# Modulation vectors: each finished half written to its row in DRAM by one four-partition transfer, two pieces later

## The chip, the cores and the metric

One core of one Trainium2 chip runs the whole program. The time is device microseconds of one execution. PE is TensorE's matrix multiplication, PEld its weight load, DVE VectorE, ACT ScalarE, POOL GpSimd, and SP the engine that issues most of the transfers. TensorE's clock is granted at one of two levels, 1.2 and 2.4 GHz; the profile writes it as a share of full speed, so 0.50 is the lower level all through a stretch.

## The reference, cut to what matters

Two blocks of two layers each, over 512 tokens of width 1024, in fp32; shown is a layer of the second. A normalisation is followed by a scale and a shift, a branch by a gate; these are vectors of 1024 that come from a conditioning vector `c` by matrix products (the first block has three of them in a layer):

```python
mod = cond @ ada_w[i] + ada_b[i]                  # cond = silu(c), 1024 long
sh1, sc1, g1, sh2, sc2, g2 = split(mod, 6)        # vectors of 1024
h = modulate(rms_norm(x, norm1_g[i]), sh1, sc1)
x = x + g1 * mixer(h)
h = modulate(rms_norm(x, norm2_g[i]), sh2, sc2)
x = x + g2 * sq_relu_mlp(h, mlp_w1[i], mlp_w2[i])
```

The first block has an even mixer (latent attention and sliding-window attention) and an odd mixer (differential and forgetting attention). The second has a convolution module, an MLP, a gated linear recurrence and another MLP. The products of these branches with their weights are most of the work. The modulation vectors themselves are small sums over large weights: the 16 rows of 1024 that this change touches take 128 loads of 512 KB.

## The kernel before, in words

fp32 operands are split into a high and a low part and multiplied in three terms, with TensorE at L209 (`mm`, `sc`, `tp`, `tq`, `pv` are PSUM tiles). A weight tile is loaded by SP (L215, or L1203 in the MLP) into `raw`, rounded by ScalarE into `hl` (L223) and its remainder taken by VectorE or GpSimd (L226, L202).

A **modulation row** is made by `ada()` (L488 to L567). A row is two halves of 512, a half four *pieces*. A piece is one load of 256x512 floats (512 KB, L498, tile `araw`, two buffers; for 24 of the 128 pieces, late in the second block, `raw` with four) and the sums over it. In most stages VectorE does them into `acc` (L547 for the first, L549 for the other seven of a half); in the convolution stage TensorE does, by small products into a PSUM tile (L525) that VectorE adds (L527). After the fourth piece come the bias (loaded by L503 into `arow`, two buffers; with TensorE doing the products it is loaded with the first piece), for VectorE's sums a product with ones over the partitions (L555), the bias added (L557), and in some rows `g` loaded into `gr` (L509) and multiplied in (L510). Then `arow` holds the half in partitions 0, 32, 64 and 96, 128 floats each, and L513 writes it to the row in DRAM. When both halves of a row are there, `spread` (L591) loads it back, broadcast over 128 partitions, into a tile `rows`, which the normalisations read (L608, L609, L759).

The pieces stand in a list `pend`. The stages call `tick`, `group` and `flush` at fixed places of their own loops to pop some, so the pieces are sown among other work: `later` issues one piece's load, and `ada_do(ADA_LAG)` does the sums of the piece before it (a lag of one). `flush` does all that is left.

**What sets the order.** The program is written for a scheduler: the order in which the code emits instructions is only its input. It simulates a timeline and puts each engine's instructions into an order of its own; each engine then runs its list strictly in that order and waits at whatever is not ready. So SP runs weight loads, pieces, biases and row writes in one fixed list; if a row write waits for `arow`, all loads behind it wait too. The two `araw` buffers let a piece's load be issued only when the sums of the piece two before it are done, and the two `arow` buffers let a bias be loaded only when the write of the half two before it has landed. Besides, SP's and ACT's transfers take eight completion counters in turn, in the order of the two lists together: a transfer on a counter waits until the one that used it before has landed.

In the convolution stage ACT also stores `u` to DRAM (`ud`, L1359) and loads it back shifted in four transfers (L1362), which TensorE multiplies at L1372.

Of the kernel before, what the change touches and what calls it, by code (L numbers as in the profile page):

```python
# [16 lines left out]
P = 128  # L17
# [87 lines left out]
def cap(base, off, dims):  # L105
    return bass.AP(tensor=base.tensor, offset=base.offset + off, ap=[list(base.ap[0])] + [list(d) for d in dims])


def cap4(v, o):

    return bass.AP(tensor=v.tensor, offset=v.offset + o, ap=[[P, 4], [0, 32], [1, P]])


class K:
    def __init__(self, tc, h, es):
        self.tc, self.nc, self.h = tc, tc.nc, h
        nc = self.nc
        pool = lambda name, bufs=1, **kw: es.enter_context(tc.tile_pool(name=name, bufs=bufs, **kw))
        self.cp = pool("cp")
        self.wp = pool("wp")  # L120
        self.rp = pool("rp")
        self.sp = pool("sp")
        self.ps = pool("ps", space=PSUM)
        self.dp = pool("dp", space=bass.MemoryType.DRAM)
        self.n = 0
        self.pend = []
        self.wn, self.lo_pool = 0, 0
        self.ada_pool = ()
        self.ada_pe, self.ada_late, self.ada_ps = False, [], "tq"
        self.ada_tag, self.ada_raw = "mm", ("araw", 2)  # L130
        self.ng, self.tick_every = 0, 1
        self.alts, self.turn = {"hn": ["tq"], "lv": ["sc", "tp"]}, {}
        self.cst = self.cp.tile([P, C_N], F32, name="cst")
        nc.scalar.dma_start(out=self.cst[:, :P], in_=h["cst"][:, :P])
        self.ident = self.cst[:, C_ID:C_ID + P]
        self.ones = self.cp.tile([P, P], F32, name="ones")
        nc.vector.memset(self.ones, 1.0)
        self.mhalf = self.cp.tile([P, 1], F32, name="mhalf")
        nc.vector.memset(self.mhalf, -0.5)
        self.dve, self.pe = nc.cur_bb.bb.instructions[-1].engine, nc.tensor.engine  # L140
        self.mark()
        self.act = [self.cp.tile([P, KC, T], F32R, name=n) for n in ("hTh", "hTl")]
# [345 lines left out]
    def ada(self, ccol, w, b, c0, kind, g=None):  # L488

        nc = self.nc  # L490
        row = self.dp.tile([D], F32, name=self.nm("row"))
        st = {}

        def load(half, gk):
            o0 = c0 + half * 512
            tag, n = self.ada_raw
            raw = self.wp.tile([P, 2, 512], F32, tag=tag, name=self.nm(tag), bufs=n)
            nc.sync.dma_start(out=raw, in_=w[gk * 256:(gk + 1) * 256, o0:o0 + 512].rearrange("(k p) c -> p k c", p=P))  # L498
            return raw

        def bias(half):
            arow = self.rp.tile([P, P], F32, tag="arow", name=self.nm("arow"), bufs=2)
            nc.sync.dma_start(out=arow, in_=cap4(b, c0 + half * 512))  # L503
            return arow

        def finish(half, arow):
            if g is not None:
                gr = self.rp.tile([P, P], F32, tag="gr", name=self.nm("gr"), bufs=2)
                nc.sync.dma_start(out=gr, in_=cap4(g, half * 512))  # L509
                nc.vector.scalar_tensor_tensor(out=arow, in0=arow, scalar=1.0 if kind == "scale" else 0.0, in1=gr,  # L510
                                               op0=ALU.add, op1=ALU.mult)
            for j in range(4):
                nc.sync.dma_start(out=row[half * 512 + j * P:half * 512 + (j + 1) * P].unsqueeze(0), in_=arow[32 * j:32 * j + 1])  # L513

        def step_pe(half, gk):

            if gk == 0:
                st[half] = bias(half)
            raw = load(half, gk)

            def products():
                ps = self.psum(self.ada_ps)
                for k in range(2):
                    for j in range(4):
                        nc.tensor.matmul(ps[32 * j:32 * j + 32, :P], lhsT=cap(ccol, gk * 2 + k, [(0, 32)]),  # L525
                                         rhs=raw[:, k, j * P:(j + 1) * P], start=k == 0, stop=k == 1, tile_position=(0, 32 * j))
                nc.vector.tensor_tensor(out=st[half], in0=ps[:, :P], in1=st[half], op=ALU.add)  # L527
                if gk == 3:
                    finish(half, st[half])

            self.ada_late.append(products)
            self.ada_do(ADA_LAG)

        def step(half, gk):
            if gk == 0:
                st[half] = self.rp.tile([P, 512], F32, tag="acc", name=self.nm("acc"), bufs=1)
            acc = st[half]
            raw = load(half, gk)
            self.ada_late.append(lambda: sums(half, gk, acc, raw))
            self.ada_do(ADA_LAG)  # L540

        def sums(half, gk, acc, raw):
            for k in range(2):
                c = ccol[:, gk * 2 + k:gk * 2 + k + 1]
                eng = nc.gpsimd if half in self.ada_pool else nc.vector
                if gk + k == 0:
                    eng.tensor_scalar(out=acc, in0=raw[:, k], scalar1=c, scalar2=None, op0=ALU.mult)  # L547
                else:
                    eng.scalar_tensor_tensor(out=acc, in0=raw[:, k], scalar=c, in1=acc, op0=ALU.mult, op1=ALU.add)  # L549
            if gk < 3:  # L550
                return
            arow = bias(half)
            ps = self.psum(self.ada_tag)
            for j in range(4):
                nc.tensor.matmul(ps[32 * j:32 * j + 32, :P], lhsT=self.ones[:, :32], rhs=acc[:, j * P:(j + 1) * P],  # L555
                                 start=True, stop=True, tile_position=(0, 32 * j))
            nc.vector.tensor_tensor(out=arow, in0=ps[:, :P], in1=arow, op=ALU.add)  # L557
            finish(half, arow)

        def later(h_, q_):  # L560
            if STRICT:
                self.mark()
            with self.tc.issue_after(self.gate):
                (step_pe if self.ada_pe else step)(h_, q_)

        self.pend += [(lambda h=h_, q=q_: later(h, q)) for h_ in range(2) for q_ in range(4)]
        return row  # L567
# [10 lines left out]
            self.tick()  # L578

    def ada_do(self, keep):  # L580
        while len(self.ada_late) > keep:
            self.ada_late.pop(0)()

    def flush(self):
        self.tick(len(self.pend))
        with self.tc.issue_after(self.gate):
            self.ada_do(0)
# [1262 lines left out]
```

## Time and profile before

| what | value |
|---|---|
| median of 3 runs | 2065.84 us (2062.28 to 2066.19) |
| the profiled execution | 2068.12 us, of it 2066.3 us span |
| granted TensorE clock, mean | 0.969 |
| PE busy | 1949.3 us (94%) |
| DVE, ACT, POOL busy | 1332.6, 895.7, 713.3 us |
| chain that ended last | PE 58%, DVE 10%, issue 6%, DMA 4% |
| row writes at L513 | 128 of 0.5 KB (32 halves, four each) |
| pieces (L498) | 128 of 512 KB |

The busy time of PE is 94% of the span, so what another engine does matters only where PE waits for it, and PE's idle time is 117 us in all (2066.3 - 1949.3). A mean clock of 0.969 is some 128 us of the span at the lower level ((1 - 0.969) / 0.5 x 2066.3).

### The profile page before, as it was taken

What the parts mean: (1) busy time and instruction counts of PE and PEld (TensorE: products, weight loads), DVE (VectorE), ACT (ScalarE), POOL (GpSimd) and SP (SyncE); (2) the same over time, 40 slices, a digit from 0 to 9 for tenths busy, and PEclk for the clock granted to TensorE, in tenths of its full rate; (3) what the DMA queues carried; (4) which work ended last, traced back from release to release, by engine and by line L of the source; (5) the groups of instructions that cost most, each with busy time, mean ns of one, the idle gap of its engine ahead of it and who ended that gap; (6) DMA issues with size and microseconds to landing.
All of it is one profiled execution on the core that took longest, in us unless ns stands there. A gap on an engine that the chain in (4) does not pass through costs nothing.

```text
span 2066.3 us, 33224 instructions
## 1 busy us (share of the span) xinstructions
PE 1949.3 (94%) x13047; PEld 1593.6 (77%) x13047; DVE 1332.6 (64%) x1996; ACT 895.7 (43%) x1561; POOL 713.3 (35%) x603
## 2 busy tenths in 40 slices
PE   7799999799999999989899999999999988999998
PEld 5687767677766786559788989877887678898896
DVE  4346675566643469647887748647676858476673
ACT  4345554145533441143424436354566524353453
POOL 1232342232333213015132331446676443323222
PEclk9899989899989999999999999999999998999999
DMA  8484456378751336842555225453322422242331
GB/s 312 133 212 145 145 174 164 93 177 155 126 126 57 134 115 201 217 123 62 185 157 168 83 82 184 134 151 105 108 78 89 142 89 75 74 133 72 123 102 62
DMA packets 230548, 272.13 MB, mean 132 GB/s; under 512 B 26874, under 2 KB 154073, under 8 KB 230392
## 3 DMA queue, kind: packets, MB, share of 16 engines
q1 hardware_dynamic: 192630, 233.88, 39.4%
q10 hardware_dynamic: 37762, 36.13, 5.9%
q8 instruction: 103, 1.69, 0.3%
q14 instruction: 53, 0.43, 0.1%
HBM read 253.57 MB, written 16.40 MB: 131 GB/s over the span
## 4 chain that ended last, share of the span: by engine, by line
PE 58%; DVE 10%; issue 6%; DMA 4%; ACT 2%; POOL 2%; DVEq 0%; POOLq 0%; ACTq 0%; SPq 0%
PE mm L209 33%; PE sc L209 6%; PE mm L1234 4%; PE sc L1234 3%; PE tp L1234 3%; PE sc L1372 2%; DVE hl L202 2%; DVE acc L549 1%; DMA araw<-in_ada_w_dram 1%; PE pv L209 1%; DVE hl L226 1%; PE tp L670 1%; DMA raw<-in_od_w_in_dram 1%; PE pv L689 1%; PE tq L209 1%
## 5 line engine op out<-in xcount | busy, mean ns | idle before, releaser
L209 PE MATMUL mm<-hTh,hl 128*128 128x512 f32 (+2 forms) x1200 | 375.0, 386 | 1.2 <-DVE b L205 1.0
L223 ACT CAST hl<-raw 128x1024 fp32r<-128x1024 f32 (+3 forms) x219 | 224.2, 1033 | 241.1 <-PE mm L209 101.9
L209 PE MATMUL mm<-hl,hid 128*128 128x512 f32 x1344 | 317.2, 395 | 3.6 <-DVE hid L202 2.0
L209 PEld LDWEIGHTS mm<-hl,hid 128*128 128x128 f32 x1344 | 252.1, 188 | 63.2 <-DVE hid L202 3.0
L226 DVE TENSOR_TENSOR hl<-raw,hl 128x1024 fp32r<-128x1024 f32 (+2 forms) x187 | 238.9, 1288 | 49.4 <-ACT hl L223 48.3
L209 PEld LDWEIGHTS mm<-hTh,hl 128*128 128x128 f32 (+1 forms) x1200 | 219.8, 190 | 50.9 <-issue 6.9
L209 PE MATMUL mm<-hl,hTh 128*128 128x256 f32 (+3 forms) x848 | 214.9, 335 | 20.9 <-DVE t L628 12.7
L209 PE MATMUL mm<-hTl,hl 128*128 128x512 f32 (+2 forms) x600 | 229.9, 383 | 0.0
L1151 POOL TENSOR_TENSOR xr<-xr,t 128x512 f32<-128x512 f32 x56 | 80.9, 1445 | 303.7 <-DVE t L1148 302.4
L209 PEld LDWEIGHTS mm<-hl,hTh 128*128 128x128 f32 x848 | 149.1, 196 | 37.4 <-DVE t L628 13.1
L549 DVE SCALAR_TENSOR_TENSOR acc<-araw,ccol,acc 128x512 f32<-128x512 f32 x154 | 135.2, 878 | 31.3 <-DMA araw<-in_ada_w_dram 24.9
L647 POOL TENSOR_TENSOR s<-s,sm 128x256 f32<-128x256 f32 (+3 forms) x112 | 81.2, 726 | 206.0 <-DVE sm L643 198.3
L201 ACT CAST hl<-raw 128x1024 fp32r<-128x1024 f32 x84 | 86.9, 1048 | 138.8 <-PE mm L209 111.5
L202 DVE TENSOR_TENSOR hl<-raw,hl 128x1024 fp32r<-128x1024 f32 x84 | 133.5, 1604 | 13.8 <-ACT hl L201 13.1
L209 PE MATMUL mm<-hl,hTl 128*128 128x256 f32 (+3 forms) x424 | 141.0, 333 | 0.7 <-DVE hTl L461 0.7
L209 PEld LDWEIGHTS mm<-hTl,hl 128*128 128x128 f32 (+1 forms) x600 | 113.8, 190 | 21.3 <-issue 1.0
L1214 POOL TENSOR_TENSOR raw<-raw,raw 128x1024 f32<-128x1024 f32 x28 | 77.0, 2749 | 146.0 <-DVE rows L1214 91.9
L226 POOL TENSOR_TENSOR hl<-raw,hl 128x1024 fp32r<-128x1024 f32 x32 | 79.2, 2476 | 103.1 <-ACT hl L223 103.0
L642 ACT ACTIVATE s<-s,sm 128x256 f32<-128x256 f32 (+5 forms) x128 | 69.5, 543 | 93.3 <-DVE sm L640 85.8
L1148 DVE TENSOR_TENSOR t<-mm,rows 128x512 f32<-128x512 f32 x56 | 38.5, 687 | 105.3 <-PE mm L209 105.2
L392 POOL TENSOR_TENSOR sm<-sm,mhalf 128x1 f32<-128x1 f32 x48 | 34.7, 722 | 203.8 <-ACT sm L387 160.7
L209 PE MATMUL sc<-b,b 64*128 64x256 f32 (+7 forms) x384 | 92.1, 355 | 2.7 <-DVE sm L640 2.1
(366 smaller groups left out, 4081.1 us busy)
## 6 DMA issues: line engine op xcount, KB each, us to landing
raw<-in_mlp_w_dram SPq DMA_DIRECT2D x128, 512.0 KB
araw<-in_ada_w_dram SPq DMA_DIRECT2D x72, 512.0 KB
raw<-in_hgrn_w_in_dram SPq DMA_DIRECT2D x40, 512.0 KB
araw<-in_w_ada_dram SPq DMA_DIRECT2D x32, 512.0 KB
raw<-in_od_w_in_dram SPq DMA_DIRECT2D x32, 512.0 KB
raw<-in_ada_w_dram SPq DMA_DIRECT2D x24, 512.0 KB
rows<-row SPq DMA_DIRECT2D x16, 512.0 KB
raw<-in_conv_w_in_dram SPq DMA_DIRECT2D x16, 512.0 KB
```

Of the source, the lines that this page charges most:

```text
L201: nc.scalar.copy(out=hi, in_=src)
L202: nc.vector.tensor_tensor(out=lo, in0=src, in1=hi.bitcast(F32), op=ALU.subtract)
L209: self.nc.tensor.matmul(out, lhsT=lt[a], rhs=rt[b], start=start and n == 0, stop=stop and n == 2)
L223: self.nc.scalar.copy(out=hi, in_=raw[:, :n])
L226: eng.tensor_tensor(out=lo, in0=raw[:, :n], in1=hi.bitcast(F32), op=ALU.subtract)
L549: eng.scalar_tensor_tensor(out=acc, in0=raw[:, k], scalar=c, in1=acc, op0=ALU.mult, op1=ALU.add)
L642: nc.scalar.activation(out=s[:, :m], in_=s[:, :m], func=AF.Exp, scale=-1.0, bias=mn, accum_out=sm)
L647: nc.gpsimd.tensor_tensor(out=p, in0=p, in1=r.to_broadcast([P, n]), op=ALU.mult)
L1151: eng.tensor_tensor(out=xs, in0=xs, in1=t, op=ALU.add)
L1214: eng.tensor_tensor(out=out, in0=x, in1=y, op=f)
L1234: nc.tensor.matmul(ps[:, m * 256:m * 256 + 256], lhsT=ws[n][:, a, k, m * P:m * P + P], rhs=parts[n][b][:, k], start=m + k + t == 0, stop=m ...
L1372: nc.tensor.matmul(ps[32 * q:32 * q + 32], lhsT=dg[:, q * 8 + i], rhs=u4[:, q, 4 * i:4 * i + T], start=i == 0, stop=i == 7, tile_position= ...
```

## The change

The four transfers of one partition each become one transfer of four partitions (0, 32, 64 and 96). It is no longer emitted where the half is finished, but put into a list with the length that `pend` shall have fallen to, which is two less; `ada_do` emits it then, before the sums that it does, and `flush` emits all that are left, before and after the last sums. Nothing else is edited; lines from L583 on stand 4 lines further down.

```diff
@@ __init__
-        self.ada_pe, self.ada_late, self.ada_ps = False, [], "tq"
+        self.ada_pe, self.ada_late, self.ada_ps, self.ada_rows = False, [], "tq", []
@@ finish, in ada
-            for j in range(4):
-                nc.sync.dma_start(out=row[half * 512 + j * P:half * 512 + (j + 1) * P].unsqueeze(0), in_=arow[32 * j:32 * j + 1])
+            self.ada_rows.append((len(self.pend) - 2, lambda: nc.sync.dma_start(
+                out=row[half * 512:half * 512 + 512].rearrange("(j c) -> j c", c=P), in_=arow[0:P:32])))
@@ ada_do
     def ada_do(self, keep):
+        while self.ada_rows and (not keep or len(self.pend) <= self.ada_rows[0][0]):
+            self.ada_rows.pop(0)[1]()
         while len(self.ada_late) > keep:
             self.ada_late.pop(0)()
+        while self.ada_rows and not keep:
+            self.ada_rows.pop(0)[1]()
```

SP's list goes from 630 transfers to 534. What the scheduler makes of it is seen in the order of the engines' lists; three places are shown. Numbers behind a name count tiles and differ between the two programs by a constant shift.

**SP in the odd mixer, about 564 us of the span** (`raw`: weights of the odd mixer, `araw`: pieces, `arow`: biases), before:

```order
L215 DMA raw_6447<-in_od_w_in_dram 128x8x128
L513 DMA row_3739<-arow_5728 1x128 x4
L498 DMA araw_6023<-in_ada_w_dram 128x2x512
L215 DMA raw_6524<-in_od_w_in_dram 128x8x128
L498 DMA araw_6027<-in_ada_w_dram 128x2x512
L503 DMA arow_6813<-in_ada_b_dram 128x1x128
L498 DMA araw_6032<-in_ada_w_dram 128x2x512
L498 DMA araw_6240<-in_ada_w_dram 128x2x512
```

and now:

```order
L215 DMA raw_6402<-in_od_w_in_dram 128x8x128
L512 DMA row_3715<-arow_5689 4x128
L503 DMA arow_6768<-in_ada_b_dram 128x1x128
L498 DMA araw_5980<-in_ada_w_dram 128x2x512
L215 DMA raw_6479<-in_od_w_in_dram 128x8x128
L498 DMA araw_5985<-in_ada_w_dram 128x2x512
L498 DMA araw_5990<-in_ada_w_dram 128x2x512
L498 DMA araw_6194<-in_ada_w_dram 128x2x512
```

The write stands at the same place among the loads; the bias, which stood behind two pieces, now stands directly behind the write and ahead of both.

**SP in the convolution stage, about 800 us of the span** (`gr`: a vector g, `raw`: weights of the convolution module; araw_7919 before is araw_7868 now), before:

```order
L215 DMA raw_8220<-in_conv_w_in_dram 128x4x256
L513 DMA row_7270<-arow_7426 1x128 x4
L498 DMA araw_7818<-in_ada_w_dram 128x2x512
L498 DMA araw_7868<-in_ada_w_dram 128x2x512
L503 DMA arow_7917<-in_ada_b_dram 128x1x128
L215 DMA raw_8687<-in_conv_w_out_dram 128x2x512
L509 DMA gr_9460<-in_norm_g_dram 128x1x128
L498 DMA araw_7919<-in_ada_w_dram 128x2x512
L498 DMA araw_7965<-in_ada_w_dram 128x2x512
```

and now:

```order
L215 DMA raw_8162<-in_conv_w_in_dram 128x4x256
L498 DMA araw_7766<-in_ada_w_dram 128x2x512
L512 DMA row_7222<-arow_7378 4x128
L498 DMA araw_7817<-in_ada_w_dram 128x2x512
L509 DMA gr_9400<-in_norm_g_dram 128x1x128
L215 DMA raw_8627<-in_conv_w_out_dram 128x2x512
L503 DMA arow_7866<-in_ada_b_dram 128x1x128
L498 DMA araw_7868<-in_ada_w_dram 128x2x512
L498 DMA araw_7910<-in_ada_w_dram 128x2x512
```

The write has moved behind one piece load, `gr` ahead of the bias, and the bias to the place directly ahead of the third piece; the pieces' own order is the same.

**DVE at the end of the even mixer, about 300 to 325 us** (`s`, `sm`: softmax of the sliding window; `oT`: the mixer's output split for the product that follows; acc_3831 before is acc_3807 now, and the last three pieces, araw_3896, 3972 and 4038, are 3872, 3948 and 4014), before:

```order
L549 SCALAR_TENSOR_TENSOR acc_3831<-araw_3832,ccol_93,acc_3831 128x512
L549 SCALAR_TENSOR_TENSOR acc_3831<-araw_3896,ccol_93,acc_3831 128x512 x2
L695 SCALAR_TENSOR_TENSOR o_754<-pv_3071,o_754 128x512
L202 TENSOR_TENSOR oT_3303<-o_754,oT_3302 128x512 x4
L549 SCALAR_TENSOR_TENSOR acc_3831<-araw_3972,ccol_93,acc_3831 128x512
L202 TENSOR_TENSOR oT_3303<-o_754,oT_3302 128x512 x3
L549 SCALAR_TENSOR_TENSOR acc_3831<-araw_3972,ccol_93,acc_3831 128x512
L226 TENSOR_TENSOR hl_836_3348<-raw_3346,hl_836_3348 128x1024
L226 TENSOR_TENSOR hl_838_3353<-raw_3351,hl_838_3353 128x1024
L226 TENSOR_TENSOR hl_840_3358<-raw_3356,hl_840_3358 128x1024
L202 TENSOR_TENSOR oT_3303<-o_754,oT_3302 128x512
L549 SCALAR_TENSOR_TENSOR acc_3831<-araw_4038,ccol_93,acc_3831 128x512 x2
```

and now:

```order
L549 SCALAR_TENSOR_TENSOR acc_3807<-araw_3872,ccol_93,acc_3807 128x512
L647 RECIPROCAL sm_3188<-sm_3187 128x1
L549 SCALAR_TENSOR_TENSOR acc_3807<-araw_3948,ccol_93,acc_3807 128x512
L644 ISA s_3198,sm_3199<-sc_3194,cst,nsink 128x256
L644 ISA sm_3199 128x1
L549 SCALAR_TENSOR_TENSOR acc_3807<-araw_3948,ccol_93,acc_3807 128x512
L647 RECIPROCAL sm_3201<-sm_3200 128x1
L549 SCALAR_TENSOR_TENSOR acc_3807<-araw_4014,ccol_93,acc_3807 128x512 x2
L699 SCALAR_TENSOR_TENSOR o_754<-pv_3052,o_754 128x512
L202 TENSOR_TENSOR oT_3279<-o_754,oT_3278 128x512 x7
L226 TENSOR_TENSOR hl_836_3324<-raw_3322,hl_836_3324 128x1024
L226 TENSOR_TENSOR hl_838_3329<-raw_3327,hl_838_3329 128x1024
```

The sums of the pieces, which stood among and behind the output splits, have moved ahead of them, in part ahead of the last softmax. All over the program 422 of DVE's rows and 1271 of PE's stand elsewhere than before, by at most 12 and 57 places.

## Rows read from the trace of the kernel before

**Rows 1.** The page of the profile: part 1, and the chain that ended last by engine (part 4).
```profile
PE 1949.3 (94%) x13047; PEld 1593.6 (77%) x13047; DVE 1332.6 (64%) x1996; ACT 895.7 (43%) x1561; POOL 713.3 (35%) x603
...
PE 58%; DVE 10%; issue 6%; DMA 4%; ACT 2%; POOL 2%; DVEq 0%; POOLq 0%; ACTq 0%; SPq 0%
```

**Rows 2.** Waits of SP's DMA queue (engine, line, waited for: us in total, times, longest).
```profile
SPq L513 <- DVE arow L557: 95.5, 14, 16.9
...
SPq L513 <- DVE arow L510: 37.9, 10, 8.3
...
SPq L503 <- DMA row<-arow: 12.7, 12, 5.1
...
SPq L498 <- DMA u<-ud: 9.1, 2, 6.9
```

**Rows 3.** Source line 513: operation, count, duration ns min/median/max, first and last start.
```profile
L513 SPq DMA_DIRECT2D row<-arow x128: 211/248/1857, 152.0 to 1667.2; - x128
```

**Rows 4.** Timeline of SP, 798 to 832 us (start, us of issuing, line, transfer, count).
```profile
800.59 1.18 SPq L513 DMA_DIRECT2D row<-arow  x4
801.87 2.15 SPq L498 DMA_DIRECT2D araw<-in_ada_w_dram  x2
...
814.27 1.07 SPq L498 DMA_DIRECT2D araw<-in_ada_w_dram  x2
```

**Rows 5.** Chain of waits, 798 to 885 us, in order of time (start, us, what).
```profile
806.01 8.20 DMA u<-ud
...
814.27 5.96 DMA araw<-in_ada_w_dram
```

**Rows 6.** Timeline of PE, 800 to 830 us (in brackets the idle time before, and its releaser).
```profile
808.49 1.08 PE L525 MATMUL tp<-araw,ccol 128*32 128x128 f32 x32
...
820.37 1.08 PE L525 MATMUL tp<-araw,ccol 128*32 128x128 f32 x16 [3.62 <-DMA araw<-in_ada_w_dram]
...
827.91 2.33 PE L1372 MATMUL sc<-u,dg 128*32 128x512 f32 x17
```

**Rows 7.** Busy time by stretch (PE, PEld, DVE, ACT, POOL, then granted clock, DMA share, GB/s).
```profile
289.70:313.60 23.90, 23.19 (x94) 15.20 (x94) 17.88 (x44) 13.04 (x35) 6.41 (x12) 0.50 0.64 203
818.70:825.60 6.90, 5.23 (x39) 3.43 (x40) 5.01 (x9) 1.05 (x1) 0.16 (x2) 0.51 0.91 318
```

**Rows 8.** Chain of waits, 404 to 440 us.
```profile
406.95 6.09 DMA raw<-in_od_w_in_dram
...
413.10 4.08 DMA araw<-in_w_ada_dram
...
419.20 9.07 DMA raw<-in_od_w_in_dram
```

**Rows 9.** Timeline of SP, 560 to 580 us.
```profile
564.30 2.73 SPq L513 DMA_DIRECT2D row<-arow  x4
567.57 0.71 SPq L498 DMA_DIRECT2D araw<-in_ada_w_dram  x1
...
573.19 0.55 SPq L503 DMA_DIRECT2D arow<-in_ada_b_dram  x1
```

**Rows 10.** Timeline of DVE, 566 to 590 us.
```profile
574.52 1.54 DVE L549 SCALAR_TENSOR_TENSOR acc<-araw,ccol,acc 128x512 f32<-128x512 f32 x2 [5.08 <-DMA araw<-in_ada_w_dram]
```

**Rows 11.** Timeline of SP, 836 to 862 us.
```profile
843.12 1.88 SPq L513 DMA_DIRECT2D row<-arow  x4
850.26 0.55 SPq L503 DMA_DIRECT2D arow<-in_ada_b_dram  x1
```

**Rows 12.** Timeline of SP, 1060 to 1085 us.
```profile
1070.46 1.12 SPq L513 DMA_DIRECT2D row<-arow  x4
1072.65 0.40 SPq L498 DMA_DIRECT2D araw<-in_ada_w_dram  x1
```

**Rows 13.** Part 5 of the page: the sums of the pieces on VectorE (busy, mean ns | idle before, releaser).
```profile
L549 DVE SCALAR_TENSOR_TENSOR acc<-araw,ccol,acc 128x512 f32<-128x512 f32 x154 | 135.2, 878 | 31.3 <-DMA araw<-in_ada_w_dram 24.9
```

**Rows 14.** Timeline of DVE, 285 to 330 us.
```profile
328.81 1.41 DVE L759 SCALAR_TENSOR_TENSOR t<-mm,sm,rows 128x512 f32<-128x512 f32 x2 [9.33 <-POOL sm L392]
```

## The prediction

> **What bounds the kernel now.** The page comes first [rows 1]. PE is busy 94% of the span, and of the chain that ended last 58% is PE, 10% DVE, 4% transfers, and SP's queue 0%. So whatever SP does with row writes is not itself on the path; it can matter only at the few places where a load that SP issues late lets PE run dry. The second view is the list of SP's waits [rows 2]. The row writes are where SP stands longest of all that this change touches: 95.5 + 37.9 = 133.4 us, in 24 waits for `arow` to be ready. To that come 12.7 us, in 12 waits, in which a bias load waits for a row write to land, and 9.1 us, in two, in which a piece load waits for transfers of `u` that have nothing to do with it. The third view is the issuing itself [rows 3]: 128 issues of 0.248 us median, 1.18 us or so for the four of a half [rows 4].
>
> Then I looked for places where a late piece stops PE. There is one that the profile names: at 816.7 us PE stands 3.62 us for `araw` [rows 6], and TensorE's clock is at 0.51 from 818.7 to 825.6 us afterwards [rows 7]. The other place is in the chain: from 406.95 to 428 us it is raw, araw, raw, three transfers in a row [rows 8].
>
> **The change, part by part.**
>
> *Fewer issues.* A half's four issues take 1.18 us; one single issue of SP takes 0.40 to 0.57 us [rows 4, 11, 12]. That is about 0.7 us less for each of 32 halves, 22 us of SP's time. SP is idle in waits for hundreds of microseconds, and its queue is 0% of the chain [rows 1], so I take 0 for it by itself. If that cover were not there, at most 22 us would be gained.
>
> *Two pieces later.* This should take the 133.4 us of waiting [rows 2] off the loads that stand behind. It does not. The scheduler had already put the writes about two loads late, and in the new list 30 of the 32 stand behind the same number of loads as before, the other two one load away, one either way. The first and the second excerpt above are one of each kind. So this part is worth nothing, and I expect about the same wait at the write.
>
> *Counters.* Four writes took four of the eight completion counters, one takes one. So all transfers behind meet other predecessors. At 800 us SP issues two pieces, a bias, a weight and `gr`, and then does nothing until 814.27 [rows 4]. The chain says why: the load of `u` is issued at 806.01, lands at 814.21, and the piece goes off 0.06 us later [rows 5]. Its buffer was free much earlier: the products that read the earlier pieces ran at 808.49 and ended at about 809.5 [rows 6]. In the new program that piece, araw_7868, waits for earlier pieces and for PE alone, so it can be issued at about 809.5 instead of 814.27: 4.8 us sooner. It took 5.96 us to land with the transfer of `u` already over [rows 5]; beside `u` it may take up to 8.2, as long as `u` itself. That lands it at 815.5 to 817.7, where PE wants it at 816.75. Of the 3.62 us of idle time between 2.7 and all is gone; I take 3.6. The stretch at 0.51 follows on that idle, and at full clock its 6.9 us of work would have taken 6.9 x 0.49 = 3.4 us less. I take that too: sum **-7.0**, bounds -2.7 and -7.0. From there to the products with `u` at 827.91 the timeline of PE shows no other idle [rows 6], so I see nothing that gives this back at once.
>
> At 413.10 the piece is issued when raw, issued at 406.95, has landed (6.09 us, to 413.04) [rows 8]; it needs nothing of it but its counter. In the new program the counter is one of a transfer that landed earlier, so it can go off right behind the write, at about 411.3: **-1.8**. It would share the queue with that raw; the bounds are 0 and -2.2 (413.10 less 410.9, the end of a single write's issue).
>
> *Biases behind the write.* This is new and costs. A bias that stands directly behind a write, as in the first excerpt, waits until the half's write has landed, because its buffer is the one that is read, and the two pieces behind it wait with it. Eight halves have this now that had not. What such a wait costs was seen once in a busy stretch: write at 843.12, bias at 850.26, so 7.1 us from write to bias [rows 11]. The mean of the 12 waits is 1.06 us [rows 2]. In the odd mixer the write is at 564.30 and the piece at 567.57 [rows 9]; with a landing after L us and a bias issue of 0.55 the piece goes off at 564.3 + L + 0.6, which is L - 2.7 later. L lies between about 1.5 (issue and mean wait) and 7.1: 0 to 4.4 us. Of those I take the middle, **+2.2**, since the queue there is neither empty nor as full as at 843. It counts, since DVE stands 5.08 us for that piece [rows 10]. At 1070.46 the same: the piece was issued at 1072.65 [rows 12], and the bias could go at 1073.72 at the latest, so 0 to 1.7 us; I take **+1.0**. For the other six I take nothing; the pieces behind them were held by their buffers anyway.
>
> *Other order on DVE.* 422 of its rows have moved, the sums of pieces mostly towards the front, past softmax work. In the third excerpt the last pieces stand ahead of the output splits. DVE waits 24.9 us in all for pieces at L549 [rows 13]; where a piece is late, the softmax behind it is late too. On the other side DVE idles 9.33 us before L759 at the end of that mixer [rows 14], so that work moved ahead leaves a gap smaller there. I take 0, bounds +8 (a third of the 24.9 once more, on the path) and -12 (half of the 23.9 us at clock 0.50 from 289.7 to 313.6 [rows 7], if that stretch came out unthrottled).
>
> *The broadcast loads* at the end of the even mixer now stand behind three pieces. Their reader is L759 at 328.81, after 9.33 us of idle [rows 14] for another releaser; that covers them, and without the cover a piece each, some 4 us [rows 8], would be due.
>
> **Sum:** -7.0 - 1.8 + 2.2 + 1.0 = **-5.6 us**. The profiled execution took 2068.12 us, so 2062.5 for one like it; it lies 2.3 us above the median of the runs, 2065.84, which less 5.6 is **2060.2 us**.
>
> One rule speaks against expecting more: the Trainium skill, "DMA: Bandwidth & Descriptors", rules for kernel authors, says that the fixed cost of a transfer overlaps when it is issued early and waited for late. By it merging four transfers would give nothing, 2065.8. The trace agrees as far as SP's 0% of the chain goes [rows 1].
>
> **Rivals.** A difference of 0.2%, 4 us, is about what a measurement of this kernel can tell from no change.
>
> 1. *No change.* The write was off the path, and what the earlier piece at 809.5 gains is taken back by `u`: both then share a queue that is busy 0.91 of the time [rows 7], `u` lands later, and PE's idle moves from the piece to `u`. For it: the 0.91. Against it: `u` landed at 814.21 [rows 5], while L1372 reads it only at 827.91 [rows 6]. Then only -2.7 to 0 is left with the +3.2 of the biases: 2065 to 2067. This is also the result if the merged write does not do what it says, which for the delay the lists already show.
>
> 2. *Slower, by DVE's new order.* In the even mixer each softmax stands behind sums whose pieces come through two buffers. If a piece needs more time than the softmax work between two pieces, DVE waits in order, the scores' consumers come late, and PE idles. It decides where pieces arrive less often than about one in 3 us; the pieces at 413.10 took 4.08 and those at 567.57 some 7 us to land [rows 8, 10]. Price: one more wait like the longest here, 5.08 [rows 10], and a throttled stretch after it, such as 6.9 x 0.49 = 3.4 [rows 7], 8.5 in all, and the +3.2 of the biases, against -1.8 and a conv gain of -2.7: 2065.84 + 7.2 = 2073. For it: the sums moved forward in 422 rows. Against it: the scheduler's order before had the same kind of waits, and they cost PE little.
>
> 3. *Larger gain.* The stretch at 289.7 comes out at full clock: -12 on top, 2048.
>
> **Numbers.** Forecast (-3 to -9 us) 0.40, its own range 2056 to 2064; rival one 0.27; rival two 0.25; rival three 0.08. Faster by over 0.2%: 0.40 + 0.08 = 0.48; within 0.2%: 0.27; slower: 0.25. The likeliest is 2060.2. The range takes in all but the tails: 2049 at the bottom, 2073 at the top.
>
> **What would show it.** `row<-arow` 32 times and SP's wait at it still above 100 us; the wait of L498 for `u` gone; a piece issued at about 809.5 and no idle of PE near 816; the clock of 800 to 850 us at 1.00. Biases: L503's wait for row writes up from 12.7 to 20 us or more. Wrong it would be if that wait of PE stays, or moves to `u`, or if new idle of PE shows in 160 to 320 us behind softmax.

## The result, and the profile after

The changed kernel takes **2099.81 us** in the median (2098.29 to 2102.42), the kernel before, beside it, 2064.06 (2061.79 to 2066.19): a ratio of 1.0172, 95% interval 1.0158 to 1.0187. It is slower by 36 us. Forecast were 2060.2 us and a range of 2049 to 2073; the time lies outside.

The page of the changed kernel, part 1 and the chain by engine [rows 1]:

```profile
PE 1959.3 (93%) x13047; PEld 1601.0 (76%) x13047; DVE 1329.2 (63%) x1996; ACT 897.0 (43%) x1561; POOL 718.1 (34%) x603
...
PE 55%; DVE 10%; DMA 6%; issue 6%; ACT 2%; POOL 2%; DVEq 0%; SPq 0%; POOLq 0%; ACTq 0%
```

PE is busy 10 us longer and the span is 30 us longer, so PE is idle for 20 us more. On the chain, transfers went from 4% to 6%. SP's issuing did become what the change promised. Source line 512, and SP's waits (who, for what: us, times, longest) [rows 2, 3]:

```profile
L512 SPq DMA_DIRECT2D row<-arow x32: 514/527/1778, 153.0 to 1693.5; - x32
```

```profile
SPq L512 <- DVE acc L547: 55.2, 6, 18.8
...
SPq L512 <- DVE arow L557: 41.2, 6, 13.3
SPq L498 <- DMA araw<-in_ada_w_dram: 38.6, 15, 8.5
SPq L503 <- DMA row<-arow: 38.5, 21, 4.1
SPq L512 <- DVE arow L510: 35.8, 10, 5.6
```

There are 32 writes of 0.53 us for 128 of 0.25. SP still stands 55.2 + 41.2 + 35.8 = 132.2 us at them, as forecast (133.4 before); with the smaller rows of that view it is 141 us, before 134. What grew are the waits of biases for a write to land, 12.7 to 38.5 us, and of pieces for earlier pieces, 22.7 to 38.6. The wait of pieces for `u` has fallen from 9.1 to 1.3 us.

**Where the 30 us arise.** PE executes the same matrix products in both profiles, so each can be looked up in both and its start compared. The difference of the two starts in us, at a few times of the profile before; each column is a single execution, and the columns e1 to e9 belong to the experiments below:

| at, us before | place | after | e1 | e3 | e4 | e5 | e6 | e7 | e8 | e9 |
|---|---|---|---|---|---|---|---|---|---|---|
| 133 | ahead of the attention | +0.9 | +2.3 | +1.5 | +2.3 | +2.9 | +1.9 | +2.7 | +2.5 | +1.9 |
| 335 | end of the even mixer | +7.8 | +2.5 | -0.1 | +11.9 | +3.2 | +1.0 | +3.1 | +9.5 | +8.8 |
| 430 | odd mixer begins | +4.9 | +2.9 | -2.2 | +10.3 | +3.1 | +4.8 | +3.2 | +9.0 | +6.1 |
| 530 | in the odd mixer | +26.8 | +2.7 | +19.8 | +12.1 | +20.3 | +5.6 | +2.4 | +9.6 | +7.4 |
| 635 | odd mixer done | +26.3 | -1.3 | +22.0 | +9.8 | +15.4 | +5.2 | -6.8 | +10.9 | -1.8 |
| 1110 | after the convolution and MLP | +25.3 | -2.1 | +24.5 | +9.1 | +16.5 | +4.7 | -4.9 | +12.3 | -1.3 |
| 2030 | end | +30.2 | -0.9 | +24.0 | +11.6 | +15.6 | +3.9 | -3.6 | +15.5 | +0.5 |

So the loss has two places: some 5 us in the even mixer, some 21 us in the odd one, most of it between 470 and 530 us. The convolution stage, from which I expected -7, gives 1 us at most. The 5 us behind 1110 gather in small steps and were not followed.

**The odd mixer.** SP's timeline there, then DVE's and PE's (in brackets the idle time before, and its releaser):

```profile
480.58 0.48 SPq L215 DMA_DIRECT2D raw<-in_od_w_in_dram  x1
481.61 0.37 SPq L498 DMA_DIRECT2D araw<-in_ada_w_dram  x1
...
514.20 0.52 SPq L512 DMA_DIRECT2D row<-arow  x1
514.77 0.55 SPq L509 DMA_DIRECT2D gr<-in_norm_g_dram  x1
517.01 0.37 SPq L498 DMA_DIRECT2D araw<-in_ada_w_dram  x1
517.48 0.55 SPq L503 DMA_DIRECT2D arow<-in_ada_b_dram  x1
518.08 0.47 SPq L215 DMA_DIRECT2D raw<-in_od_w_in_dram  x1
518.99 4.30 SPq L498 DMA_DIRECT2D araw<-in_ada_w_dram  x2
537.92 0.37 SPq L215 DMA_DIRECT2D raw<-in_od_w_in_dram  x1
```

```profile
495.62 0.75 DVE L549 SCALAR_TENSOR_TENSOR acc<-araw,ccol,acc 128x512 f32<-128x512 f32 x1 [6.96 <-DMA araw<-in_ada_w_dram]
...
536.01 0.75 DVE L549 SCALAR_TENSOR_TENSOR acc<-araw,ccol,acc 128x512 f32<-128x512 f32 x1 [12.63 <-DMA araw<-in_ada_w_dram]
```

```profile
498.25 0.41 PE L674 MATMUL tp<-cst,s 128*128 128x128 f32 x2 [3.93 <-DVE s L1050]
...
538.35 1.32 PE L209 MATMUL sc<-b,b 64*128 64x384 f32 x3 [8.13 <-DVE sm L644]
```

Two stalls of DVE, 6.96 and 12.63 us, for pieces; softmax stands behind these sums in DVE's list, and PE runs dry for 3.93 and 8.13 us. The piece of the first stall was issued at 481.61, directly behind the weight `raw` at 480.58. The piece of the second was issued at 518.99, and DVE got it at 536; just ahead of it in SP's list stands `raw` at 518.08. In the kernel before, each of the two was issued ahead of its weight. DVE waited 0.91 us for the first. At the second place SP and DVE did this, in the kernel before:

```profile
501.55 1.41 SPq L498 DMA_DIRECT2D araw<-in_ada_w_dram  x2
503.14 0.56 SPq L503 DMA_DIRECT2D arow<-in_ada_b_dram  x1
503.80 0.42 SPq L215 DMA_DIRECT2D raw<-in_od_w_in_dram  x1
```

```profile
505.47 0.75 DVE L549 SCALAR_TENSOR_TENSOR acc<-araw,ccol,acc 128x512 f32<-128x512 f32 x1 [2.06 <-DMA araw<-in_ada_w_dram]
...
509.29 0.99 DVE L549 SCALAR_TENSOR_TENSOR acc<-araw,ccol,acc 128x512 f32<-128x512 f32 x1
```

The 2.06 us are for the piece ahead of the one in question; for that one, at 509.29, DVE did not wait. What the transfer engines do meanwhile shows in the busy times by stretch [rows 7] (PE, PEld, DVE, ACT, POOL, clock, DMA share, GB/s); the last row is a stretch of the convolution stage, for comparison:

```profile
284.10:321.60 37.50, 35.94 (x146) 23.23 (x146) 27.47 (x72) 18.71 (x53) 12.43 (x23) 0.50 0.63 193
520.50:530.00 9.50, 9.50 (x41) 6.75 (x40) 2.44 (x5) 2.43 (x6) 0.00 (x0) 1.00 1.03 44
840.00:847.00 7.00, 3.66 (x30) 2.52 (x28) 6.07 (x11) 0.00 (x0) 0.00 (x0) 1.00 1.06 290
```

From 520.5 to 530 us the engines are busy all the time (a share of 1.03) and move 44 GB/s; at 840 us, equally busy, 290. The weights of this mixer's heads are loads of 8x128 columns, rows of 512 bytes in DRAM; a piece has rows of 2 KB. The first row is the even mixer: the stretch at the lower clock is 37.5 us long, where it was 23.9 [rows 7]. 13.6 us more at half the clock are 6.8 us of work lost, which is the loss there (from +0.9 to +7.8 in the table). Why that stretch lasts longer is not parted further: ahead of it, from 240 us on, PE's longest idle is 1.04 us, for DVE's softmax.

**The convolution stage** [rows 4 to 6]: SP's timeline, the chain, and PE's:

```profile
827.22 0.52 SPq L512 DMA_DIRECT2D row<-arow  x1
827.83 0.39 SPq L498 DMA_DIRECT2D araw<-in_ada_w_dram  x1
...
834.43 1.15 SPq L498 DMA_DIRECT2D araw<-in_ada_w_dram  x2
```

```profile
827.83 6.55 DMA araw<-in_ada_w_dram
...
834.43 11.59 DMA araw<-in_ada_w_dram
```

```profile
834.52 0.64 PE L525 MATMUL tp<-araw,ccol 128*32 128x128 f32 x16 [1.30 <-DVE ol L1357]
...
846.16 0.65 PE L525 MATMUL tp<-araw,ccol 128*32 128x128 f32 x16 [3.14 <-DMA araw<-in_ada_w_dram]
```

The piece no longer waits for `u`; now it waits for the piece before, which takes 6.55 us, goes off among the loads of `u` (833.26 to 835.1), and takes 11.59 us instead of 5.96. PE's idle is 1.30 + 3.14 us instead of 3.62.

### The profile page after: what moved, and what is told of

Read it like the earlier page. It is cut to its first block, busy times and chain, and to the rows that moved or that the text cites. A ratio compares the mean times of both kernels' runs of the same rounds, so it can differ in the third digit from the quotient of the medians.

```text
span 2096.5 us, 33109 instructions
## 1 busy us (share of the span) xinstructions
PE 1959.3 (93%) x13047; PEld 1601.0 (76%) x13047; DVE 1329.2 (63%) x1996; ACT 897.0 (43%) x1561; POOL 718.1 (34%) x603
## 3 DMA queue, kind: packets, MB, share of 16 engines
q1 hardware_dynamic: 192630, 233.88, 38.6%
## 4 chain that ended last, share of the span: by engine, by line
PE 55%; DVE 10%; DMA 6%; issue 6%; ACT 2%; POOL 2%; DVEq 0%; SPq 0%; POOLq 0%; ACTq 0%
PE mm L209 31%; PE sc L209 6%; PE mm L1238 4%; DMA araw<-in_ada_w_dram 3%; PE sc L1238 3%; PE tp L1238 3%; DVE acc L549 2%; PE sc L1376 2%; DVE hl L202 2%; DMA raw<-in_mlp_w_dram 1%; PE pv L209 1%; DVE hl L226 1%; PE tp L674 1%; PE pv L693 1%; POOL xr L1762 1%
## 5 line engine op out<-in xcount | busy, mean ns | idle before, releaser
L209 PE MATMUL mm<-hl,hTh 128*128 128x256 f32 (+3 forms) x848 | 220.6, 342 | 20.7 <-DVE t L632 12.5
L202 DVE TENSOR_TENSOR hl<-raw,hl 128x1024 fp32r<-128x1024 f32 x84 | 133.4, 1602 | 13.6 <-ACT hl L201 12.8
L209 PE MATMUL sc<-b,b 64*128 64x256 f32 (+7 forms) x384 | 95.2, 363 | 12.3 <-DVE sm L644 11.8
```

What stands on the lines that cost most here:

```text
L202: nc.vector.tensor_tensor(out=lo, in0=src, in1=hi.bitcast(F32), op=ALU.subtract)
L209: self.nc.tensor.matmul(out, lhsT=lt[a], rhs=rt[b], start=start and n == 0, stop=stop and n == 2)
```

## The experiments

Theory A after the result: the single write costs nothing; the loss is the **order** into which the scheduler put everything else because of it. Rival B: the single write itself is slow, or what waits for its landing (the biases), or the counters.

The tool for it is a list. Each engine's order is taken from one of the two built kernels and given to the scheduler as edges between neighbours. They force the order and add no wait:

```diff
     with tile.TileContext(nc, schedule_with_timeline_sim=True) as tc:
         build(tc, args)
+        replay(tc, nc)
...
+def replay(tc, nc):
+    for eng, order in ORDERS.items():
+        for a, b in zip(order, order[1:]):
+            tc.add_manual_dep(b, a.name, DependencyInfo(NoSync, DATA), reason="replay")
```

**e1, one write, old order on all engines.** `ORDERS` of before; a half's one write stands where its four stood.

> The changed kernel's 32 single writes, but all five engines are held to the order of the kernel before (edges between neighbours, no waits added); the four writes of a half stand as one where the four stood. Theory A (the loss is the scheduler's new order): the time of the kernel before, 2064 us, between 2056 and 2070; the 12.6 us and 7.0 us stalls of DVE for pieces in the odd mixer are gone. Rival B (the loss is the one write itself: it lands later, or the counters that moved with it cost): 2090 to 2102.

Measured: 2064.08 us, ratio 0.9988 (0.9974 to 1.0003). The loss is gone, all of it. B falls for the write and the counters: merging the writes is worth nothing that can be told from zero, and costs nothing. The biases keep their old places here, so of them e1 says nothing; e6 does.

**e2, four writes, new order on all engines.** The code of before, `ORDERS` of the changed kernel.

> The kernel before with its 128 writes, but all five engines held to the order of the changed kernel; the four writes of a half stand where the one stands. Theory A: the time of the changed kernel, 2095 to 2112 us (SP issues four writes again, some 22 us of its time, mostly hidden). Rival B: 2060 to 2072.

Measured: 2105.10 us, ratio 1.0193 (1.0176 to 1.0210). The order alone, without the change, has the whole loss.

**e3 and e4, whose order it is.** e3: SP's list new, the others old. e4: SP's list old, the others new.

> One write; SP's list in the order of the changed kernel, PE, DVE, ACT and POOL in the order of the kernel before. If SP's order carries the loss (weight loads with short rows ahead of pieces, biases directly behind writes): 2085 to 2105 us. If DVE's order carries it (sums of pieces ahead of softmax): 2060 to 2072.

> One write; SP's list in the order of the kernel before, PE, DVE, ACT and POOL in the order of the changed kernel. If DVE's order carries the loss: 2085 to 2105 us. If SP's order does: 2060 to 2072. If it takes both, e3 and e4 lie between, and their losses add up to some 35 us.

Measured: e3 2093.53 us, ratio 1.0134 (1.0119 to 1.0150); e4 2080.72 us, 1.0073 (1.0058 to 1.0088). It takes both, and the table parts them by place: SP's list costs in the odd mixer (e3: +24 us from 430 to 635) and nothing in the even one, the lists of the compute engines cost 9 to 10 us in the even mixer and nothing in the odd one. The two losses add up to 43 us by the ratios, more than the changed kernel's 36, so they are not terms of a sum. Which of the four lists of e4 costs was not parted. e4's even mixer has the stretch at the lower clock too, 41.0 us long; with SP's new list, in the changed kernel, it is 37.5:

```profile
285.40:326.40 41.00, 37.46 (x149) 23.97 (x149) 27.06 (x72) 19.49 (x53) 11.97 (x23) 0.50 0.60 170
```

**e5 and e6, which rows of SP's list.** e5 is e1 with two weights moved, as the changed kernel has them; e6 is e1 with only the biases and the loads of `g` moved:

```diff
 L512 row_3714<-arow_4768
+L215 raw_5505<-in_od_w_in
 L498 araw_4984
 L503 arow_5393
 L498 araw_5058
-L215 raw_5505<-in_od_w_in
...
 L498 araw_5315
+L215 raw_5746<-in_od_w_in
 L498 araw_5384
 L503 arow_5689
-L215 raw_5746<-in_od_w_in
```

> e1 (one write, old order on all engines) with two weight loads alone moved on SP as in the changed kernel: raw_5505 ahead of its two pieces, raw_5746 ahead of one. If it is these two (rows of 512 bytes, slow to arrive) that hold the pieces back: 8 to 20 us over e1, so 2072 to 2084 us, and DVE's waits for pieces in the odd mixer up from 13 to over 25 us. If it is the biases: e1's time, 2060 to 2068.

> e1 with only the bias and g loads moved on SP to where the changed kernel has them (counted in loads from the write), weights and pieces in the old order. If the wait of a bias for the write's landing holds up the pieces, as my prediction had it: 3 to 15 us over e1, so 2067 to 2079 us. If the weights alone do it: e1's time, 2060 to 2068.

Measured: e5 2084.60 us, ratio 1.0074 (1.0047 to 1.0101); e6 2072.94 us, 1.0030 (1.0015 to 1.0045). By ratios against e1, the two weights cost 0.86%, 18 us, and the biases with the loads of `g` 0.42%, 9 us; with the intervals of both ratios that is roughly 11 to 24 and 4 to 13 us. The first is the larger cause, and DVE's waits for pieces in the odd mixer are 27.6 us in e5 against 12.9 in e1. The second, of which I had the biases in the sum, is real. e5's DVE shows the stalls of the changed kernel at the same two pieces:

```profile
490.19 0.75 DVE L549 SCALAR_TENSOR_TENSOR acc<-araw,ccol,acc 128x512 f32<-128x512 f32 x1 [5.47 <-DMA araw<-in_ada_w_dram]
...
530.63 0.75 DVE L549 SCALAR_TENSOR_TENSOR acc<-araw,ccol,acc 128x512 f32<-128x512 f32 x1 [9.63 <-DMA araw<-in_ada_w_dram]
```

In e6 the bias of the first excerpt waits as forecast:

```profile
569.91 1.98 SPq L512 DMA_DIRECT2D row<-arow  x1
576.19 0.54 SPq L503 DMA_DIRECT2D arow<-in_ada_b_dram  x1
576.83 0.42 SPq L498 DMA_DIRECT2D araw<-in_ada_w_dram  x1
```

The bias goes off 6.3 us behind the write, the piece 6.9; in e1 the piece goes off 3.3 us behind it (567.04 and 570.30). Against e1's profile, e6 loses 3.7 us from 580 to 590 us, behind this place. Another 4.3 us arise between 335 and 350 us and were not followed; some of it is made up later, and the profile has 5 us of the 9 at its end.

**e8, the two weights put back in the changed kernel,** the rest as it is.

> The changed kernel in its own order on all engines, only the two weight loads of e5 put back behind their pieces on SP. If they carry the loss in the odd mixer: 2078 to 2090 us, 10 to 20 under the changed kernel's 2099.8. If the biases do: 2095 to 2103.

Measured: 2082.81 us, ratio 1.0071 (1.0056 to 1.0086), by the ratios 1.0% or 21 us under the changed kernel. By place (table) it stands at +9.5 us at the end of the even mixer and at +10.9 behind the odd one: the odd mixer's loss is all but gone, the even mixer's is left.

**e9, rows of 2 KB instead of 512 bytes.** The changed kernel in its own order; the 16 weight loads of 8x128 columns fetch 2x512 columns, so the odd mixer works on other numbers:

```diff
+        wide = nk == 8 and cw == 128 and w.tensor is self.h["od_w_in"].tensor
         self.nc.sync.dma_start(
-            out=raw[:, :n].rearrange("p (k c) -> p k c", c=cw),
-            in_=w[k0 * P:(k0 + nk) * P, c0:c0 + cw].rearrange("(k p) c -> p k c", p=P))
+            out=raw[:, :n].rearrange("p (k c) -> p k c", c=512 if wide else cw),
+            in_=(w[:2 * P, c0 // 512 * 512:c0 // 512 * 512 + 512] if wide else
+                 w[k0 * P:(k0 + nk) * P, c0:c0 + cw]).rearrange("(k p) c -> p k c", p=P))
```

> The changed kernel in its own order on all engines; the 16 weight loads of the odd mixer that fetch 8x128 columns (rows of 512 bytes) fetch as many bytes as 2x512 columns (rows of 2 KB) instead, from another place of the same matrix, so the odd mixer's products are of other numbers. If it is the short rows that make these loads slow and the pieces behind them late: 2075 to 2085 us, 15 to 25 under the changed kernel, with DVE's waits for pieces in the odd mixer below 15 us (36.5 now). If the loads are late for another reason (their place alone, the amount of bytes): 2092 to 2102.

Measured: 2069.48 us, ratio 1.0018 (1.0003 to 1.0033): by the ratios 1.5% or 32 us under the changed kernel, more than expected. DVE's waits for pieces in the odd mixer are 12.1 us instead of 36.5. The odd mixer, in the changed kernel and in e9 (same columns as above):

```profile
440.00:625.00 185.00, 160.40 (x863) 124.54 (x863) 101.11 (x239) 77.75 (x160) 52.92 (x46) 0.91 0.66 122
```

```profile
440.00:600.00 160.00, 153.98 (x879) 119.43 (x878) 101.01 (x242) 78.94 (x162) 57.00 (x49) 1.00 0.52 144
```

The transfer engines are busy 0.52 of the time instead of 0.66 and move more, 144 GB/s instead of 122, and the clock is at full speed throughout. So an unlucky place of a weight in SP's list costs as much as it does because this weight is slow. The rows of e9 are longer and also lie elsewhere (two groups of 128 rows of the matrix instead of eight, and loads of neighbouring columns fetch the same bytes); no run parts these. But the changed kernel's trace speaks against the length alone. From 578.76 to 591.18 us SP issues three weights of this kind and nothing else, and while they arrive the rate changes:

```profile
588.00:590.00 2.00, 2.00 (x12) 1.30 (x11) 0.46 (x2) 0.71 (x2) 0.00 (x0) 1.00 1.00 47
590.50:593.00 2.50, 2.50 (x20) 1.87 (x18) 2.24 (x3) 0.91 (x2) 2.10 (x1) 1.00 1.07 186
```

In both stretches nearly all that moves are rows of 512 bytes, at 47 GB/s in one and 186 in the other. Such a load is slow for a part of its time, and what makes it so is open.

The Trainium skill, "DMA: Bandwidth & Descriptors", section "Why small descriptors are slow (HBM only)", gives a packet a fixed overhead of about 3 cycles beside one cycle for each 32 bytes. An estimate by it for rows of 512 bytes is 16 / 19, or 84% of the full rate. The trace has 44 GB/s against 290, so that overhead alone does not explain these loads, and the measurement decides.

**e12, the same in the kernel before.**

> The kernel before in its own order, with the 16 weight loads of e9 fetching rows of 2 KB from another place of the same matrix (the odd mixer's products are of other numbers). If short rows already hold pieces back in the kernel before: its DVE waits of 14.9 us in the odd mixer fall below 5 us, the throttled stretch at 586 us goes as in e7, and the time is 5 to 12 us under the kernel before, 2054 to 2062. If only the changed order suffers from them: 2063 to 2070.

Measured: 2058.38 us, ratio 0.9961 (0.9946 to 0.9977). The kernel before suffers from these loads too, by some 8 us. DVE's waits for pieces fell from 14.9 to 8.1 us, not below 5. Between e9 and e12, both with the loads of 2 KB rows, the changed order still costs 0.57%, 12 us. e12's row for the odd mixer, ahead of it that of the kernel before:

```profile
435.00:600.00 165.00, 157.97 (x869) 121.18 (x869) 102.37 (x242) 78.39 (x161) 56.05 (x48) 0.96 0.70 139
```

```profile
435.00:600.00 165.00, 161.18 (x926) 125.00 (x927) 107.49 (x255) 81.99 (x170) 57.37 (x50) 1.00 0.50 142
```

**e7 and e10, a weight moved the other way.** e7 is e1 with one weight of 8x128 columns behind a piece that stood behind it; e10 is the kernel before with its four writes and the same move:

```diff
 L498 araw_5980
-L215 raw_6479<-in_od_w_in
 L498 araw_5985
+L215 raw_6479<-in_od_w_in
 L503 arow_6768
```

> e1 with one weight load, raw_6479 (the one at 568 us), moved the other way, behind the second piece. If slow weight loads ahead of a piece are what makes DVE wait: 3 to 9 us under e1, 2055 to 2061 us (DVE's wait of 5.4 us at 577 to 583 gone, and the throttled stretch from 586.6 us shorter). If not: e1's time or slower, since the weight comes later.

> The kernel before, four writes a half, old order on all engines, and only raw_6479 behind the second piece as in e7. If e7's gain is the moved weight's: 4 to 9 us under the kernel before, 2057 to 2062. If it needs the single write: 2063 to 2068.

Measured: e7 2062.22 us, ratio 0.9971 (0.9956 to 0.9987); e10 2063.93 us, 0.9986 (0.9971 to 1.0002). e7 lies 0.29% under the kernel before; under e1, of which it is an edit, it lies 0.17% by the ratios, 4 us, which their intervals do not part from nothing. At its place it shows the mechanism backwards: DVE's wait for the second piece, 5.43 us in the kernel before and 4.30 in e1, is gone, and a stretch of 18 us runs at full clock. The wait in the kernel before, and then the stretch in the kernel before, e1, e7 and e10:

```profile
583.05 0.75 DVE L549 SCALAR_TENSOR_TENSOR acc<-araw,ccol,acc 128x512 f32<-128x512 f32 x1 [5.43 <-DMA araw<-in_ada_w_dram]
```

```profile
583.00:601.00 18.00, 15.22 (x47) 9.20 (x46) 7.55 (x19) 5.95 (x14) 11.02 (x9) 0.62 0.45 90
586.00:604.00 18.00, 16.18 (x76) 10.01 (x76) 7.20 (x20) 7.44 (x16) 10.98 (x9) 0.81 0.42 89
586.00:604.00 18.00, 18.00 (x104) 12.51 (x102) 9.31 (x26) 8.47 (x19) 10.43 (x10) 1.00 0.46 101
585.00:603.00 18.00, 17.83 (x100) 12.30 (x99) 9.53 (x28) 10.73 (x22) 11.41 (x10) 1.00 0.50 106
```

e10 has the same stretch at full clock with four writes, so at its place the gain needs no single write. Its time falls into the band that was set for the other case and cannot be told from no change. That the move makes the whole program faster is not shown. A kernel that fetches these weights in longer rows and computes the reference was not tried.

**e11, one write without the delay.**

```diff
-            self.ada_rows.append((len(self.pend) - 2, lambda: nc.sync.dma_start(
-                out=row[half * 512:half * 512 + 512].rearrange("(j c) -> j c", c=P), in_=arow[0:P:32])))
+            nc.sync.dma_start(out=row[half * 512:half * 512 + 512].rearrange("(j c) -> j c", c=P), in_=arow[0:P:32])
```

> The changed kernel without the delay: one write, emitted where the half is finished. The scheduler gives the same lists as for the changed kernel on all engines, but for one piece and one write that change places on SP in the convolution stage. All theories: the changed kernel's time, 2095 to 2104 us; were the delay worth something, it would differ by over 6 us.

Measured: 2100.08 us, ratio 1.0164 (1.0136 to 1.0191), the changed kernel's time. "Issued two pieces later" changes nothing; the merged write alone brings the new lists (the two programs have the same order on every engine but for one pair of rows). Why the scheduler answers so was not studied.

## Why the prediction was wrong

- *Fewer issues, 0.* Right: e1 is within 0.3% of the kernel before, on the good side if any. The rule of the Trainium skill that I weighed ("DMA: Bandwidth & Descriptors", rules for kernel authors: the fixed cost overlaps) agrees with e1's 0.9988, as far as the merging as such goes.
- *Two pieces later, 0.* Right, by e11; and the wait at the write stayed, 132.2 us.
- *Counters, -7.0 and -1.8.* The wait went as said, the time did not come. In e1, with the old order, the piece is issued at 808.25 instead of 814.27:

```profile
799.32 0.53 SPq L512 DMA_DIRECT2D row<-arow  x1
799.94 0.91 SPq L498 DMA_DIRECT2D araw<-in_ada_w_dram  x2
...
808.25 1.12 SPq L498 DMA_DIRECT2D araw<-in_ada_w_dram  x2
```

```profile
808.31 0.64 PE L525 MATMUL tp<-araw,ccol 128*32 128x128 f32 x16 [0.40 <-DMA araw<-in_ada_w_dram]
...
819.79 0.64 PE L525 MATMUL tp<-araw,ccol 128*32 128x128 f32 x16 [3.66 <-DVE ol L1357]
```

  PE waits 3.66 us all the same, now for DVE, which has its own chain of `ol` to run first; in the changed kernel the piece shares the queue with `u` and takes 11.59 us. This was my first rival, with a chance of 0.27: right at this place that the shared queue takes the gain back, though the idle did not move to `u`, and wrong for the whole. I took the idle of PE as held by one wait, the counter's; the shared queue and DVE's chain ended within a few us of it. The -1.8 did not come either: the piece of 413.10 is issued 1.2 us behind its write instead of 2.7 (415.35 and 416.57 in the changed kernel), and PE's difference stays between +4.9 and +5.2 us from 400 to 430 us.
- *Biases, +3.2.* The mechanism is there: in e6 the piece behind the write of 564.30 goes off 3.6 us later behind that write than in e1, inside the bounds of 0 to 4.4. The term was too small for all places together, 9 us in e6, where the loads of `g` are moved as well. L503's waits grew by 26 us in the changed kernel, and I had given six of the eight new places nothing, on the word that buffers held the pieces there anyway, for which I showed no row.
- *Other order on DVE, 0 with bounds of +8 and -12.* This is the step that failed, in two ways. In the even mixer the lists of the compute engines cost 9 to 10 us (e4), the upper bound and a little more; that it is DVE's list among the four was not parted. And the step looked only at DVE: of **SP's own list** I compared the places of the writes and of the biases, but not the places of weights against pieces. The two that moved cost 18 us. My own rows had the sign of it: DVE stood 5.08 us for a piece [rows 10] behind weights of this kind, and a piece took 7 us there. I read that as the price of a bias, not as a queue that is slow because of what is in it. I had looked for late pieces only where PE waits for them itself. Behind DVE's waits for two pieces, 5.08 us and 5.43 at 583.05, the kernel before already ran at the lower clock from 586.6 to 600.3 us.
- *The rivals.* The second, slower by DVE's order, had the right direction and kind, DVE standing in order for a piece and a throttled stretch behind it. Its price was one such wait, 8.5 us. There were two such waits, 6.96 and 12.63 us, and the even mixer's part beside them; the range ended at one. Its "one in 3 us" was worked out from no row. The third rival had the stretch at 289.7 come out at full clock; it grew from 23.9 to 37.5 us at the lower one.
- *The chances.* A forecast of -3 to -9 us is 2057 to 2063, not 2056 to 2064, and its end of -3 lies inside the 0.2% that was given to no change.

## What to carry to other kernels

Where a scheduler orders the program, a small edit is two changes: what it does, and what it makes the scheduler do; hold the order fixed with edges and each can be timed alone. Compare the new lists of every engine, and of a loading queue all that stands in it: weights against pieces as much as the transfers that were edited. And look at what moves few bytes in a busy queue: a slow load holds up what stands behind it, and an engine that runs in order then passes the delay on.

## What the runs showed of the hardware

- Loads of 512 KB in rows of 512 bytes kept the transfer engines fully busy at 44 GB/s for 9.5 us, where others at the same share moved 290. Loads of the same shape moved 186 in another stretch, so the length of the rows is not the whole reason. With rows of 2 KB from another place the same kernel was 32 us faster by the ratios.
- A stall was paid twice in the odd mixer. Over 185 us of the changed kernel PE is idle for 24.6 us and has a clock of 0.91; over 160 us of e9 it is idle for 6.0 and has 1.00. In the even mixer no idle of PE from 240 us to the stretch at the lower clock is over 1.04 us, and yet the stretch is 37.5 us long instead of 23.9.
- One write of four partitions takes SP 0.53 us, four writes of one took 1.18.
